# A decoder layer on one core: two block pairs used plainly at the top of the way back, visits staggered by two pairs, weight sums made at once

## The chip, the core and the metric

The kernel runs on one core of a Trainium2 chip. Time is device time in microseconds (us) from the start of one execution to its end; the median of several executions is compared. The core has a matrix engine (PE, with its weight loads PEld), a vector engine (DVE), a scalar engine (ACT), a general engine (POOL) and a synchronising engine (SP). In this kernel SP and POOL also issue the transfers (DMA) between device memory and on-chip memory (SBUF). PE writes its results into eight banks of an accumulator memory (PSUM); DVE and ACT read them from there.

## What is computed

One layer of a decoder, for 512 prompt tokens and 8 × 4 sample tokens, all in 32-bit floats, with width 2048 and an MLP of width 8192. Only the MLP part matters here:

```python
h = rms_norm(x, norm_mix_w)
x = x + mixer(h, ...)                       # projections, convolutions, delta rule, w_out
h = rms_norm(x, norm_ffn_w)
x = x + jnp.square(jax.nn.relu(h @ w_up)) @ w_down    # 2048 -> 8192 -> 2048
return rms_norm(x, final_norm_w)            # and the new states
```

## The kernel before, in words

**Layout.** Activations stand with features on 128 partitions and tokens along the row. The 544 tokens are cut into two halves of 272 (256 of the prompt and 16 samples), so one matmul is 128 × 128 weights against 128 × 272 values. A 2048-wide activation is 16 blocks, or 8 pairs; the 8192-wide one is 64 blocks, or 32 pairs (`NF`), named m = 0 to 31.

**Three matmuls for one product.** PE works in a rounded 32-bit format. Each weight tile and each activation is split into a rounded part (`hi`, by ACT) and a remainder (`lo`, by DVE), and hi·hi + hi·lo + lo·hi are added up in one bank. `weight` (L106 to L122) loads a tile into `w_raw` (two buffers), and splits it into `w_hi` and `w_lo` (three buffers each). A loop called `ahead` calls the load of an item two items before its use.

**Seven products for eight.** For most pairs the MLP takes 2 × 2 blocks of weights (a11, a12, a21, a22) and 2 × 2 blocks of activations (two blocks by two token halves) and forms the four results with seven block products instead of eight, in the way of Strassen and Winograd. Class `Pair` loads the four quads of weights (tiles `w_q`) and makes sums of them on DVE: s1 = a21 + a22 (L1052), a21 = a11 − a21 (L1054), a11 = s1 − a11 (L1055), a12 = a12 − a11 (L1056). The products, numbered 1 to 7, use a11, a12, a22, ... in the order `ORDER` = 1, 2, 5, 6, 7, 3, 4, all through the matmul of L1088. Products 1, 6, 7 and 4 are collected in one bank ("x"), 5 and 3 in another ("z"), 2 in a third ("y"). Since each intermediate sum in x is itself needed, x is read out after 1, 6, 7 and 4 before the next product adds to it. In the function `bilinear` the loads of the next pair's quads are called at product 5.

**Way up.** Pairs 0 to 2 (`N_PLAIN` = 3) are computed plainly (`plain`, one token half at a time). Pairs 3 to 31 go through `bilinear`, 168 matmuls each (7 products × 8 blocks × 3). After each, `block_out` reads out the banks, applies relu and square, and `keep_sums` makes the activation sums that the way back needs and writes them, split, to device memory (`ucd`). A few pairs are stored as they are (`STORED` = 1, 2, 31). Pair 0 is split at once and kept in `u0d`. Pair 2 is read again during pair 8 (`LATER`), and its sums are made then, so that the way back can use it with the others.

**Way back.** First a plain part adds pair 0's share to all 16 blocks of the residual `x2v` (weights `w_d0`, 192 matmuls on L145, additions on DVE L897). Then 29 pairs, 2 to 30 (`KS`), are used in visits: a visit works on one of the 8 pairs of output blocks (m) and on up to `SPAN` = 6 inner pairs, with 7 × n × 3 matmuls for n pairs. The first visits of the eight outputs are staggered (`starts` = 0, 0, 1, 2, 3, 3, 4, 5), so that the inner pairs can be read in through a ring of 8 (`RING`, `fetch`, L1159, issued by POOL); 45 visits in all. Seven additions into `x2v` (L897) follow the seven products of each visit. The weight quads of the visits (`w_q`, from `w_d1`) lie in a pool `qp` that takes the memory of the pools of the way up (`tt`, `sq`), after they are closed. Last, pairs 1 and 31 are used plainly together with the final norm (`w_d2`).

**Order of the work.** The program text gives an order; a scheduler works out the order on each engine at build time from its own model of durations, from a priority (`urgent` raises it) and from when buffers come free. The order on each engine is then fixed: an instruction that has to wait for longer than the model assumed holds up all that stand behind it on that engine.

Of the kernel before, what the change touches and what calls it, by code (L numbers as in the profile page):

```python
# [18 lines left out]
P = 128  # L19
# [20 lines left out]
STORED = [1, 2, NF - 1]  # L40
SPAN, RING = 6, 8
LATER = 8
# [13 lines left out]
def trunk(ctx, tc, a):  # L56
# [835 lines left out]
    u0_d = tile_in(dram, "u0d", [P, 2, 2, 2, HT])  # L892
    uc_d = {m: tile_in(dram, f"ucd{m}", [P, 14, HT]) for m in range(2, NF - 1)}
# [71 lines left out]
    def plain(m, h):  # L965
        t = t_tile("u", "u")
        u = t[:, :2]
        for i in range(2):
            ps = ps_small(HT)
            for j in range(2):  # L970
                with urgent():
                    w = weight(a["w_up"][m, 2 * i + j], 1024)
                for k in range(KT // 2):
                    x = h_c[k][1 + j] if h == 0 else (d_c[k][0][:, j], d_c[k][1][:, j])
                    product({h: ps}, w, k * P, tuple((t, t) for t in x), j == k == 0, j == 1 and k == 7, (h,))
            with urgent():
                S.activation(u[:, i], ps, AF.Relu)
        with urgent():
            S.activation(u, u, AF.Square)
        if m:  # L980
            for i in range(2):
                nc.gpsimd.dma_start(u_d[m][:, 2 * i + 1 - h], u[:, i])
            return
        hi = t[:, 2:4].bitcast(F32R)
        parts_into(hi, u.bitcast(F32R), u)
        for i in range(2):
            nc.gpsimd.dma_start(u0_d[:, 0, i, h], t[:, 2 + i])
            nc.gpsimd.dma_start(u0_d[:, 1, i, h], u[:, i])
# [40 lines left out]
    ORDER = (1, 2, 5, 6, 7, 3, 4)  # L1029

    class Pair:
# [12 lines left out]
        def parts(self, p):  # L1044
            n = self.n
            if p in (1, 2) and self.q is None:
                return weight(self.src[p - 1], n)
            a11, a12, a21, a22 = self.q
            with urgent():
                if p == 5:  # L1050
                    self.s1 = tile_in(rawp, "w_s1", [P, 1024], tag="w_raw")[:, :n]
                    V.tensor_tensor(self.s1, a21, a22, ADD)  # L1052
                elif p == 6:
                    V.tensor_tensor(a21, a11, a21, SUB)  # L1054
                    V.tensor_tensor(a11, self.s1, a11, SUB)  # L1055
                    V.tensor_tensor(a12, a12, a11, SUB)  # L1056
                s = {1: a11, 2: a12, 6: a11, 5: getattr(self, "s1", None), 7: a21, 3: a12, 4: a22}[p]
                hi = tile_in(whip, "w_hi", [P, 1024], F32R)[:, :n]
                lo = tile_in(wlop, "w_lo", [P, 1024], F32R)[:, :n]
                S.activation(hi, s, AF.Copy)  # L1060
                V.tensor_tensor(lo, s, hi.bitcast(F32), SUB)  # L1061
            return hi, lo

    def bilinear(items, early, cs, outs):

        order = [w for w, p in items if p == 5]

        def load(it):
            w, p = it
            if w not in early or p == 5:  # L1070
                w.load()
            if p == 5:
                at = order.index(w)
                for nxt in order[at + 1 : at + 2]:
                    nxt.load()
            return w.parts(p)

        for (w, p), (whi, wlo) in ahead(items, load):
            if p == 1:
                w.ps, w.out = {"x": bank(True)}, outs(w.key)  # L1080
# [34 lines left out]
    def block_out(m):  # L1115
        u = t_tile("u", "u")

        def out(p, ps):
# [15 lines left out]
            if p == 7 and m == LATER:  # L1134
                t = g_tile("u_2", [P, 4, HT])
                nc.sync.dma_start(t, u_d[2])
                keep_sums(2, t)
            if p == 1 and m == NF - 1:
                residual(range(4), nc.sync)
            if p == 5 and m == NF - 1:  # L1140
                for i in range(2):
                    parts = [c_tile(hlp, "u0") for _ in range(2)]
                    for j in range(2):
                        nc.sync.dma_start(parts[j].bitcast(F32), u0_d[:, j, i])
                    u_0.append(tuple(parts))
            if p in (5, 6) and m == NF - 1:
                fetch(p - 5)
# [4 lines left out]
    KS = list(range(2, NF - 1))  # L1152

    def fetch(j):
        n = {4: 4, 5: 0, 6: 0, 7: 0}.get(j % RING, 7)
        n2 = n + {4: 3, 5: 7, 6: 4}.get(j % RING, 0)
# [13 lines left out]
    for j in range(2, 4):  # L1170
        fetch(j)
    x2 = [x2p[i // 2][:, i % 2] for i in range(KT)]
    for q, w in ahead(range(KT // 4), lambda q: weight(a["w_d0"][q], 1024)):
        for j in range(4):
            ob = 4 * q + j
            ps = [bank(True), bank(False)]
            for k in range(2):
                product(ps, w, (2 * j + k) * P, u_0[k], k == 0, k == 1)
            for h in range(2):
                add(x2[ob][:, h], ps[h])  # L1180
    late.close()

# [6 lines left out]
    starts = [SPAN * m // 8 for m in range(8)]  # L1189
    visits = [(m, 0, starts[m]) for m in range(8) if starts[m]]  # L1190
    at = list(starts)
# [7 lines left out]
    for j in range(4, RING):  # L1199
        fetch(j)  # L1200
# [20 lines left out]
    bilinear([(w, p) for w in downs for p in ORDER], (),  # L1221
# [4 lines left out]
    for m in (1, NF - 1):  # L1226
# [102 lines left out]
def _pack(x_prompt, x_sample, state_conv_a, state_conv_qkv, state_delta, norm_mix_w, w_in,  # L1329
# [27 lines left out]
    arr["w_d0"] = wd[:, :, 0:2].reshape(4, 4, P, 2 * P).transpose(0, 2, 1, 3).reshape(4, P, 1024)  # L1357
    w1 = wd.reshape(8, 2, P, NF, 2, P)
    arr["w_d1"] = w1.transpose(0, 1, 4, 2, 3, 5).reshape(8, 4, P, NF * P)
    w2 = wd[:, :, [2 * m + i for m in (1, NF - 1) for i in range(2)]]  # L1360
# [57 lines left out]
```

## Time and profile before

| | |
|---|---|
| median of 3 executions | 2495.59 us (2492.95 to 2500.96) |
| the profiled execution | 2508.89 us, its span 2507.1 us |
| PE | 2435.8 us busy, 97% of the span, 19065 matmuls |
| DVE | 1821.1 us, 73% |
| ACT | 1105.4 us, 44% |
| POOL | 498.3 us, 20% |
| granted PE clock, mean | 0.979 |
| DMA | 400.76 MB, 160 GB/s on average |

A page of the profile gives busy times, the clock that PE was granted, the groups of instructions and the chain of work that ended last. A timeline row gives the start in us, the duration, the engine, the line of the program, the operation, what it writes and reads, the shape, and in brackets how long the engine sat idle before it and what ended that. `xN` at the end of a timeline row means N instructions merged into one row. Matmuls overlap: a row of 0.29 us does not mean that the next one starts 0.29 us later, so pace is read from starts. Some matmul records are missing.

### The profile page before, as it was taken

To read this page: it belongs to the slowest core of one execution; us is meant where nothing else is said; L and a number is where in the kernel's file an instruction comes from. 1 tells how busy PE (TensorE), PEld (TensorE's weight loads), DVE (VectorE), ACT (ScalarE), POOL (GpSimd) and SP (SyncE) were. 2 spreads that over 40 slices of the span, in tenths; PEclk is the share of its full clock that TensorE was granted. 3 is DMA by queue.
4 is the path that set the end of the run, shared out by engine and by line. 5 is a ranking of instruction groups with operands and counts; after the bars stand their busy time and mean duration, and the time that the engine had idled before them with its cause. 6 is when DMAs were issued, how large, how long until landed. Compare 5 with 4: busy or idle time off the path is not lost.

```text
span 2507.1 us, 47369 instructions
## 1 busy us (share of the span) xinstructions
PE 2435.8 (97%) x19065; PEld 2389.9 (95%) x19065; DVE 1821.1 (73%) x2993; ACT 1105.4 (44%) x1628; POOL 498.3 (20%) x783
## 2 busy tenths in 40 slices
PE   8999999999999999999999999999899999999997
PEld 8999999999999899989999999999799999999996
DVE  8676575567557635788888888888488787878795
ACT  5425333332532524565555555555233333333346
POOL 4124113212312303310111111111401111111003
PEclk9999998999998999999999999999899999999998
DMA  6233333332423536565565555556846666566323
GB/s 197 91 106 110 94 101 98 112 97 88 135 88 92 200 106 205 187 195 200 193 228 195 195 194 189 188 190 220 320 127 195 195 195 193 191 194 193 108 84 106
DMA packets 145812, 400.76 MB, mean 160 GB/s; under 512 B 35540, under 2 KB 46456, under 8 KB 145592
## 3 DMA queue, kind: packets, MB, share of 16 engines
q1 hardware_dynamic: 109368, 265.56, 33.7%
q0 software_dynamic: 36224, 132.16, 14.6%
q8 instruction: 150, 2.46, 0.4%
q14 instruction: 70, 0.57, 0.1%
HBM read 318.76 MB, written 78.89 MB: 159 GB/s over the span
## 4 chain that ended last, share of the span: by engine, by line
PE 56%; issue 23%; DVE 9%; DMA 6%; POOL 3%; ACT 2%; SPq 0%; POOLq 0%; DVEq 0%; ACTq 0%
PE ps_big L145 25%; PE ps_s L1088 23%; PE ps_sm L145 3%; DVE w_lo L121 3%; DMA w_raw<-in_w_o_dram 2%; DMA w_raw<-in_w_up_dram 1%; POOL ucd L1106 1%; POOL ucd L1105 1%; DMA w_q<-in_w_d_dram 1%; ACT w_hi L118 1%; DVE xm L560 1%; PE ps_s L145 1%; DVE tm L556 1%; DMA tn<-ti 1%; DVE x2v L897 1%
## 5 line engine op out<-in xcount | busy, mean ns | idle before, releaser
L1088 PE MATMUL ps_s<-uc,w_hi 128*128 128x272 f32 x3248 | 621.1, 291 | 10.8 <-ACT w_hi L1060 8.3
L1060 ACT ACTIVATE w_hi<-w_q 128x768 fp32r<-128x768 f32 (+6 forms) x440 | 382.6, 873 | 544.7 <-PE ps_s L1088 395.3
L1088 PEld LDWEIGHTS ps_s<-uc,w_hi 128*128 128x128 f32 x3248 | 510.8, 189 | 20.4 <-ACT w_hi L1060 11.4
L1061 DVE TENSOR_TENSOR w_lo<-w_q,w_hi 128x768 fp32r<-128x768 f32 (+6 forms) x440 | 434.2, 989 | 61.0 <-ACT w_hi L1060 58.3
L1088 PE MATMUL ps_s<-uc,w_lo 128*128 128x272 f32 x1624 | 462.9, 289 | 0.3
L145 PE MATMUL ps_big<-x_hi,w_hi 128*128 128x272 f32 x1984 | 425.1, 294 | 0.9 <-ACT x_hi L133 0.7
L145 PE MATMUL ps_big<-x_hi,w_lo 128*128 128x272 f32 x1984 | 420.8, 292 | 2.4 <-DVE w_lo L121 2.4
L145 PE MATMUL ps_big<-x_lo,w_hi 128*128 128x272 f32 x1984 | 420.5, 293 | 0.3 <-DVE x_lo L136 0.3
L118 ACT ACTIVATE w_hi<-w_raw 128x1024 fp32r<-128x1024 f32 (+3 forms) x211 | 206.9, 980 | 402.9 <-PE ps_big L145 249.5
L121 DVE TENSOR_TENSOR w_lo<-w_raw,w_hi 128x1024 fp32r<-128x1024 f32 (+3 forms) x211 | 269.8, 1279 | 138.5 <-ACT w_hi L118 135.8
L145 PEld LDWEIGHTS ps_big<-x_hi,w_hi 128*128 128x128 f32 x1984 | 317.2, 190 | 5.0 <-issue 1.4
L145 PEld LDWEIGHTS ps_big<-x_hi,w_lo 128*128 128x128 f32 x1984 | 316.3, 191 | 3.9 <-DVE w_lo L121 3.0
L145 PEld LDWEIGHTS ps_big<-x_lo,w_hi 128*128 128x128 f32 x1984 | 315.9, 191 | 0.9 <-DVE x_lo L136 0.5
L1088 PEld LDWEIGHTS ps_s<-uc,w_lo 128*128 128x128 f32 x1624 | 304.6, 189 | 2.3 <-DVE w_lo L1061 1.9
L1088 PE MATMUL ps_s<-c_hi,w_lo 128*128 128x272 f32 x928 | 267.7, 289 | 2.2 <-DVE w_lo L1061 1.5
L1088 PE MATMUL ps_s<-c_hi,w_hi 128*128 128x272 f32 x928 | 266.6, 287 | 0.5 <-ACT w_hi L118 0.5
L1088 PE MATMUL ps_s<-c_lo,w_hi 128*128 128x272 f32 x928 | 266.3, 287 | 0.0
L1159 POOL DMA_DIRECT2D uc<-ucd x203 | 110.4, 548 | 439.5 <-PE ps_s L1088 411.0
L897 DVE TENSOR_TENSOR x2v<-x2v,ps_s 128x272 f32<-128x272 f32 x347 | 148.6, 434 | 67.5 <-PE ps_s L1088 59.1
L1088 PEld LDWEIGHTS ps_s<-c_hi,w_lo 128*128 128x128 f32 x928 | 174.4, 188 | 3.2 <-DVE w_lo L1061 2.1
L1088 PEld LDWEIGHTS ps_s<-c_hi,w_hi 128*128 128x128 f32 x928 | 174.5, 188 | 0.7 <-ACT w_hi L118 0.7
L1088 PEld LDWEIGHTS ps_s<-c_lo,w_hi 128*128 128x128 f32 x928 | 174.5, 188 | 0.0
(378 smaller groups left out, 4270.7 us busy)
## 6 DMA issues: line engine op xcount, KB each, us to landing
w_q<-in_w_up_dram SPq DMA_DIRECT2D x116, 512.0 KB, 4.3
uc<-ucd POOLq DMA_DIRECT2D x203, 272.0 KB, 5.3
w_raw<-in_w_in_dram SPq DMA_DIRECT2D x106, 512.0 KB, 3.4
w_q<-in_w_d_dram SPq DMA_DIRECT2D x128, 384.0 KB, 3.7
w_raw<-in_w_o_dram SPq DMA_DIRECT2D x32, 512.0 KB, 3.4
ucd<-u_hi POOLq DMA_DIRECT2D x29, 544.0 KB, 5.4
ucd<-tc POOLq DMA_DIRECT2D x29, 544.0 KB, 6.7
w_raw<-in_w_up_dram SPq DMA_DIRECT2D x28, 512.0 KB, 3.6
```

Source lines behind the costliest of these rows:

```text
L118: S.activation(hi[:, c], raw[:, c], AF.Copy)
L121: V.tensor_tensor(lo[:, c], raw[:, c], hi[:, c].bitcast(F32), SUB)
L145: PE.matmul(ps[h], wp[:, c : c + P], x, start=start and i == 0, stop=stop and i == 2)
L556: V.tensor_tensor(t, xm[:, :, j : j + 1].broadcast_to([P, 8, n]), um[:, j : j + 1, j + 1 :].broadcast_to([P, 8, n]), MUL,)
L560: V.tensor_tensor(xm[:, :, j + 1 :], xm[:, :, j + 1 :], t, SUB)
L897: V.tensor_tensor(out, out, ps, ADD)
L1060: S.activation(hi, s, AF.Copy)
L1061: V.tensor_tensor(lo, s, hi.bitcast(F32), SUB)
L1088: PE.matmul(ps, wp[:, k * P : (k + 1) * P], xp, start=p in (1, 2, 5) and k == j == 0, stop=k == len(c) - 1 and j == 2, skip_group_check=True,)
L1105: nc.gpsimd.dma_start(d[:, at : at + n], hi.bitcast(F32))
L1106: nc.gpsimd.dma_start(d[:, 7 + at : 7 + at + n], src)
L1159: nc.gpsimd.dma_start(t.bitcast(F32), uc_d[KS[j]][:, 2 * b : 2 * b + 2])
```

## The change

`N_PLAIN` stays 3, but pairs 0 and 1 are both kept, split, for a plain use at the top of the way back, pair 2 is stored for the end in pair 1's place, and only the 28 pairs 3 to 30 go through visits. The plain part takes 8 weight tiles of 2 output blocks × 4 inner blocks instead of 4 tiles of 4 × 2 (384 matmuls), and it is no longer a stretch of its own: it becomes items of `bilinear`, three ahead of the first visit, two after it, two after the second, one after the third. The first visits start at 0, 0, 2, 2, 4, 4, 6, 6, so there are 42 visits. Pair 2's sums during pair 8 go away, with the reading back of it. In `Pair`, products 5 and 6 change places, and all four weight sums are made at product 6, which now comes third; this holds on the way up and on the way back. The kept parts are read at product 2 of the last pair, eight tiles instead of four. The reads for the ring change their places in the pools accordingly.

```diff
@@ constants
-STORED = [1, 2, NF - 1]
+KEPT = [0, 1]
+STORED = [2, NF - 1]
-LATER = 8
+RAMP = [0, 0, 2, 2, 4, 4, 6, 6]
@@ plain
-        if m:
+        if m not in KEPT:
             for i in range(2):
                 nc.gpsimd.dma_start(u_d[m][:, 2 * i + 1 - h], u[:, i])
             return
         hi = t[:, 2:4].bitcast(F32R)
         parts_into(hi, u.bitcast(F32R), u)
         for i in range(2):
-            nc.gpsimd.dma_start(u0_d[:, 0, i, h], t[:, 2 + i])
-            nc.gpsimd.dma_start(u0_d[:, 1, i, h], u[:, i])
+            nc.gpsimd.dma_start(u0_d[m][:, 0, i, h], t[:, 2 + i])
+            nc.gpsimd.dma_start(u0_d[m][:, 1, i, h], u[:, i])
@@ Pair and bilinear
-    ORDER = (1, 2, 5, 6, 7, 3, 4)
+    ORDER = (1, 2, 6, 5, 7, 3, 4)
...
-                if p == 5:
+                if p == 6:
                     self.s1 = tile_in(rawp, "w_s1", [P, 1024], tag="w_raw")[:, :n]
                     V.tensor_tensor(self.s1, a21, a22, ADD)
-                elif p == 6:
                     V.tensor_tensor(a21, a11, a21, SUB)
                     V.tensor_tensor(a11, self.s1, a11, SUB)
                     V.tensor_tensor(a12, a12, a11, SUB)
...
         def load(it):
             w, p = it
-            if w not in early or p == 5:
+            if p == "plain":
+                return weight(*w.src)
+            if w not in early or p == 6:
                 w.load()
-            if p == 5:
+            if p == 6:
                 at = order.index(w)
                 for nxt in order[at + 1 : at + 2]:
                     nxt.load()
             return w.parts(p)

         for (w, p), (whi, wlo) in ahead(items, load):
+            if p == "plain":
+                w.run((whi, wlo))
+                continue
@@ block_out
-            if p == 7 and m == LATER:
-                t = g_tile("u_2", [P, 4, HT])
-                nc.sync.dma_start(t, u_d[2])
-                keep_sums(2, t)
             if p == 1 and m == NF - 1:
                 residual(range(4), nc.sync)
-            if p == 5 and m == NF - 1:
-                for i in range(2):
+            if p == 2 and m == NF - 1:
+                for i in range(4):
                     parts = [c_tile(hlp, "u0") for _ in range(2)]
                     for j in range(2):
-                        nc.sync.dma_start(parts[j].bitcast(F32), u0_d[:, j, i])
+                        nc.sync.dma_start(parts[j].bitcast(F32), u0_d[i // 2][:, j, i % 2])
                     u_0.append(tuple(parts))
-            if p in (5, 6) and m == NF - 1:
-                fetch(p - 5)
+            if p in (6, 5) and m == NF - 1:
+                fetch(6 - p)
@@ ring
-    KS = list(range(2, NF - 1))
+    KS = list(range(N_PLAIN, NF - 1))
     def fetch(j):
-        n = {4: 4, 5: 0, 6: 0, 7: 0}.get(j % RING, 7)
-        n2 = n + {4: 3, 5: 7, 6: 4}.get(j % RING, 0)
+        n = {3: 0, 4: 0, 5: 0, 7: 4}.get(j % RING, 7)
+        n2 = n + {3: 7, 4: 7}.get(j % RING, 0)
@@ top of the way back
-    for j in range(2, 4):
-        fetch(j)
     x2 = [x2p[i // 2][:, i % 2] for i in range(KT)]
-    for q, w in ahead(range(KT // 4), lambda q: weight(a["w_d0"][q], 1024)):
-        for j in range(4):
-            ob = 4 * q + j
-            ps = [bank(True), bank(False)]
-            for k in range(2):
-                product(ps, w, (2 * j + k) * P, u_0[k], k == 0, k == 1)
-            for h in range(2):
-                add(x2[ob][:, h], ps[h])
     late.close()
+    class Plain:
+        def __init__(self, q):
+            self.q, self.src = q, (a["w_d0"][q], 1024)
+        def run(self, w):
+            for j in range(2):
+                ob = 2 * self.q + j
+                ps = [bank(True), bank(False)]
+                for k in range(4):
+                    product(ps, w, (4 * j + k) * P, u_0[k], k == 0, k == 3)
+                for h in range(2):
+                    add(x2[ob][:, h], ps[h])
...
-    starts = [SPAN * m // 8 for m in range(8)]
-    visits = [(m, 0, starts[m]) for m in range(8) if starts[m]]
-    at = list(starts)
+    visits = [(m, 0, RAMP[m]) for m in range(8) if RAMP[m]]
+    at = list(RAMP)
...
-    for j in range(4, RING):
+    for j in range(2, RING):
         fetch(j)
...
-    bilinear([(w, p) for w in downs for p in ORDER], (),
+    items = [[(w, p) for p in ORDER] for w in downs]
+    plains = [(Plain(q), "plain") for q in range(8)]
+    items[0] = plains[:3] + items[0] + plains[3:5]
+    items[1] += plains[5:7]
+    items[2] += plains[7:]
+    bilinear([it for part in items for it in part], (),
              lambda key: [combos(key[1][1] + k) for k in range(key[1][2])], down_out)
@@ last
-    for m in (1, NF - 1):
+    for m in STORED:
```

More of the change, by code (lines that the diff above doesn't have):

```diff
@@ L891, in trunk @@
     u_d = {m: tile_in(dram, f"ud{m}", [P, 4, HT]) for m in STORED}
-    u0_d = tile_in(dram, "u0d", [P, 2, 2, 2, HT])
-    uc_d = {m: tile_in(dram, f"ucd{m}", [P, 14, HT]) for m in range(2, NF - 1)}
+    u0_d = [tile_in(dram, f"u0d{m}", [P, 2, 2, 2, HT]) for m in KEPT]
+    uc_d = {m: tile_in(dram, f"ucd{m}", [P, 14, HT]) for m in range(N_PLAIN, NF - 1)}
     def add(out, ps):
@@ L1064, in bilinear @@
     def bilinear(items, early, cs, outs):
-        order = [w for w, p in items if p == 5]
+        order = [w for w, p in items if p == 6]
         def load(it):
             w, p = it
-            if w not in early or p == 5:
+            if p == "plain":
+                return weight(*w.src)
+            if w not in early or p == 6:
                 w.load()
-            if p == 5:
+            if p == 6:
                 at = order.index(w)
@@ L1356, in _pack @@
     wd = _blocks(w_down[0])
-    arr["w_d0"] = wd[:, :, 0:2].reshape(4, 4, P, 2 * P).transpose(0, 2, 1, 3).reshape(4, P, 1024)
+    arr["w_d0"] = wd[:, :, 0:4].reshape(8, 2, P, 512).transpose(0, 2, 1, 3).reshape(8, P, 1024)
     w1 = wd.reshape(8, 2, P, NF, 2, P)
     arr["w_d1"] = w1.transpose(0, 1, 4, 2, 3, 5).reshape(8, 4, P, NF * P)
-    w2 = wd[:, :, [2 * m + i for m in (1, NF - 1) for i in range(2)]]
+    w2 = wd[:, :, [2 * m + i for m in STORED for i in range(2)]]
     arr["w_d2"] = w2.reshape(8, 2, P, 512).transpose(0, 2, 1, 3).reshape(8, P, 1024)
```

## The prediction

> **What bounds the kernel now.** The page's engine totals come first, then the matrix engine's (PE's) timeline for its pace, then the windows for the place of the lost time.
>
> ```profile
> span 2507.1 us, 47369 instructions
> PE 2435.8 (97%) x19065; PEld 2389.9 (95%) x19065; DVE 1821.1 (73%) x2993; ACT 1105.4 (44%) x1628; POOL 498.3 (20%) x783
> ```
>
> PE is occupied 97% of the span, so only matmul count and PE's gaps can move the end. Its undisturbed pace is read from the first four products of the last pair on the way up, 96 matmuls in a row, of which these are the first and the last:
>
> ```profile
> 1740.12 0.29 PE L1088 MATMUL ps_s<-c_hi,w_hi 128*128 128x272 f32 x1
> ...
> 1751.98 0.29 PE L1088 MATMUL ps_s<-c_hi,w_lo 128*128 128x272 f32 x1
> ```
>
> 11.86 us over 95 steps: 0.1248 us per matmul. Any window's length less its matmuls times 0.1248 is its loss. Columns below: stretch, length, then busy time and count of PE and of the others, granted clock, DMA share, GB/s.
>
> ```profile
> 1248.50:1312.20 63.70, 61.12 (x470) 60.15 (x469) 51.68 (x63) 35.10 (x44) 8.69 (x16) 0.97 0.62 219
> 1312.20:1376.00 63.80, 63.80 (x507) 63.19 (x506) 52.95 (x61) 37.16 (x45) 6.52 (x12) 1.00 0.57 194
> 1376.00:1741.50 365.50, 365.50 (x2895) 362.02 (x2894) 303.79 (x345) 213.14 (x259) 36.93 (x68) 1.00 0.55 193
> 1762.80:1847.00 84.20, 69.95 (x463) 65.44 (x462) 51.93 (x125) 21.15 (x41) 25.03 (x46) 0.90 0.73 261
> 1847.00:2360.00 513.00, 513.00 (x4050) 508.42 (x4049) 412.85 (x585) 190.78 (x226) 79.84 (x147) 1.00 0.57 181
> 2360.00:2437.30 77.30, 74.17 (x561) 71.02 (x559) 66.46 (x140) 32.20 (x59) 0.00 (x0) 1.00 0.30 85
> ```
>
> In order: around the delayed sums of pair 2 the loss is 63.7 − 470 × 0.1248 = 5.0 us, in the next stretch of equal length 0.5, in the steady way up 4.2 over 17 pairs, in the top of the way back (plain product and the five short visits) 26.4, in the steady visits 7.6 over 32, in the last short visits 7.3. The top of the way back is the largest, and its granted clock is 0.90.
>
> **The change, part by part.**
>
> *More matmuls.* A pair used plainly costs 8 × 48 matmuls per two pairs; the visits take 8 × 28 × 21 = 4704 instead of 8 × 29 × 21 = 4872, the plain part 384 instead of 192. Net +24 × 0.1248 = **+3.0**.
>
> *Order 1, 2, 6, 5, 7.* Products 6 and 7 use one bank, and 7 may start only when 6 has been copied out. They stand next to each other now; PE bridges the copy with matmuls of product 3, then pauses:
>
> ```profile
> 1562.26 0.28 PE L1088 MATMUL ps_s<-d_lo,w_hi 128*128 128x272 f32 x1
> 1562.53 0.39 PE L1088 MATMUL ps_s<-d_hi,w_hi 128*128 128x272 f32 x1
> 1562.76 0.29 PE L1088 MATMUL ps_s<-d_lo,w_hi 128*128 128x272 f32 x1
> ```
>
> ```profile
> 1562.09 0.38 ACT L1121 ACTIVATE u<-ps_s 128x272 f32<-128x272 f32 x1
> ```
>
> The copy ends at 1562.47 and the next matmul starts at 1562.53; the two steps take 0.50 instead of 0.25, so 0.25 us per pair. With 5 between 6 and 7 the copy has 24 × 0.1248 = 3.0 us, or 2.2 in a visit of six, against under 1.5 us from the end of 6 to the end of the copy. Products 7 and 4 stand so today, one product apart, and no gap is there. On the way up 28 × 0.25 = **−7.0** (bounds 0 and −7.5), in the visits 7.6 × 30/32 = **−7.0** (bounds 0 and −8).
>
> *All four weight sums ahead of product 6.* The third product now waits for four sums instead of one. Today's order on the vector engine (DVE), and the rounding on the scalar engine (ACT) that starts the third product:
>
> ```profile
> 1545.60 1.23 DVE L1061 TENSOR_TENSOR w_lo<-w_q,w_hi 128x1024 fp32r<-128x1024 f32 x1 [0.58 <-ACT w_hi L1060]
> ...
> 1547.09 1.22 DVE L1055 TENSOR_TENSOR w_q<-w_s,w_q 128x1024 f32<-128x1024 f32 x1
> ...
> 1549.37 1.22 DVE L1052 TENSOR_TENSOR w_s<-w_q 128x1024 f32<-128x1024 f32 x1
> 1550.50 1.22 DVE L1061 TENSOR_TENSOR w_lo<-w_s,w_hi 128x1024 fp32r<-128x1024 f32 x1
> 1551.63 1.22 DVE L1056 TENSOR_TENSOR w_q<-w_q 128x1024 f32<-128x1024 f32 x1
> 1552.77 1.22 DVE L1054 TENSOR_TENSOR w_q<-w_q 128x1024 f32<-128x1024 f32 x1
> ```
>
> ```profile
> 1549.15 1.06 ACT L1060 ACTIVATE w_hi<-w_s 128x1024 fp32r<-128x1024 f32 x1 [1.06 <-PE ps_s L1088]
> ```
>
> ```profile
> 1549.02 0.29 PE L1088 MATMUL ps_s<-c_hi,w_hi 128*128 128x272 f32 x1
> ```
>
> ACT rounds s1 at 1549.15 while DVE writes the next s1 at 1549.37: s1 and L1054 are made a whole pair ahead. Product 6 then hangs on L1055 alone, which needs the first product's `w_lo` and ends at 1548.31; the third product's buffer comes free later, at 1549.02, when the pair's first product starts on PE. Cost **0** under cover of that lead; without it, rival D. The first pair of the way up has no lead, and pays today:
>
> ```profile
> 1157.59 0.39 PE L1088 MATMUL ps_s<-d_hi,w_lo 128*128 128x272 f32 x1 [1.98 <-DVE w_lo L1061]
> ```
>
> There three sums move ahead of the third product, 3 × 1.135 = 3.4 us of DVE time, but as much of it as today must be done before the fifth; the wait comes earlier and is not larger in total: 0, bounds ±2.5.
>
> *Pair 2's sums dropped on the way up.* They used a quad buffer and `tc`:
>
> ```profile
> 1267.34 0.44 DVE L1007 TENSOR_TENSOR tc<-u 128x272 f32<-128x272 f32 x1 [2.93 <-DMA ucd<-tc]
> ...
> 1281.24 1.23 DVE L1052 TENSOR_TENSOR w_s<-w_q 128x1024 f32<-128x1024 f32 x1 [1.38 <-DMA w_q<-in_w_up_dram]
> ```
>
> ```profile
> 1283.66 0.39 PE L1088 MATMUL ps_s<-d_hi,w_lo 128*128 128x272 f32 x1 [2.08 <-DVE w_lo L1061]
> ...
> 1287.61 0.43 PE L1088 MATMUL ps_s<-d_hi,w_lo 128*128 128x272 f32 x1
> ```
>
> The loss goes from 5.0 to the neighbour's 0.5: **−4.5** (bounds −3 and −5). These rows also show what a wait costs behind itself: after 2.08 us idle PE steps at 0.226 (1283.66 to 1283.89) until 1287.8, some 2 us more. The Trainium skill, "TensorE: Matmul & The Clock Gate", section "What's actually happening", puts the halving of the clock behind an idle window of about 3.4 us. Here 2.08 us is enough, so the measurement decides; by the page the waits left at the top would be 2 us cheaper, and the sum −35.
>
> *Pair 1 kept.* It adds, per half of the tokens, a rounding, a subtraction and two more writes on POOL's queue:
>
> ```profile
> 1114.17 0.72 DVE L925 TENSOR_TENSOR u<-u 128x544 fp32r<-128x544 f32 x1
> ```
>
> ```profile
> 1113.40 0.66 ACT L924 ACTIVATE u<-u 128x544 fp32r<-128x544 f32 x1
> ```
>
> Between 0 (both steps in idle time between weight splits) and 2 × (0.66 + 0.72) = 2.8 bare, taken as **+1.0**: DVE has gaps there, but some splits will stand behind the new steps. POOL's extra writes have nothing behind them that PE waits for before the top of the way back. The four more loads of kept parts on SP go out at product 2 of the last pair, ahead of the plain weights; that traffic is in the next term.
>
> *The top of the way back.* Now a plain stretch of 24 us, then visits of 1, 2, 3, 3, 4, 5; afterwards three plains (18 us), a visit of 2, two plains, a visit of 2, two plains, a visit of 4, a plain, a visit of 4, then sixes. The reads of stored sums keep their order on POOL (0, 1, the residual, 2 and on); 6 and 7 now wait for the kept `u` until the last plain, but their first use is the ninth visit, and behind them stand only later reads: 0.
>
> ```profile
> 1762.80 0.66 PE L145 MATMUL ps_s<-u,w_hi 128*128 128x272 f32 x4
> ```
>
> ```profile
> SPq L1042 <- DMA ud<-u: 11.0, 1, 11.0
> ```
>
> ```profile
> 1774.11 1.48 DVE L897 TENSOR_TENSOR x2v<-x2v,ps_s 128x272 f32<-128x272 f32 x4
> 1783.85 0.29 DVE L1052 TENSOR_TENSOR w_s<-w_q 128x128 f32<-128x128 f32 x1 [8.27 <-DMA uc<-ucd]
> ```
>
> ```profile
> 1784.87 1.40 PE L145 MATMUL ps_s<-u,w_hi 128*128 128x272 f32 x4 [6.06 <-DVE x2v L897]
> 1786.06 0.66 PE L145 MATMUL ps_s<-u,w_lo 128*128 128x272 f32 x2
> ...
> 1805.44 0.52 PE L1088 MATMUL ps_s<-uc,w_hi 128*128 128x272 f32 x2 [3.12 <-ACT w_hi L1060]
> ...
> 1818.04 0.52 PE L1088 MATMUL ps_s<-uc,w_hi 128*128 128x272 f32 x2 [2.21 <-ACT w_hi L1060]
> ```
>
> SP's first weight quads wait until the last pair's `u` is written (`qp` lies where `u` lay), and all later loads of SP stand behind them; DVE, at the first sum, waits for them until 21.0 us after the first plain matmul (1783.85 − 1762.8); the residual additions behind it leave PE without banks for 6.06 us. The change keeps this cause: `u` is written at the same point of POOL's queue, and the first quads are twice as large. But the three plains are 144 × 0.1248 = 18.0 us of PE work in six blocks; two of them are added before DVE stops, and the four banks of each kind hold the rest. The first visit can start at 21.0 plus one split of 0.4 and the step to PE, say 22: about 4 us idle, plus the 2 of slow clock seen above. A visit of 2 costs DVE 11 weight passes and 7 additions against 42 × 0.1248 = 5.2 us of PE:
>
> ```profile
> 1807.50 1.09 DVE L1061 TENSOR_TENSOR w_lo<-w_q,w_hi 128x256 fp32r<-128x256 f32 x3
> ```
>
> 1.09/3 and 1.48/4 give 11 × 0.36 + 7 × 0.37 = 6.6: 1.4 us each, 2.8. Each plain behind a visit of 2 waits 1.06 + 1.23 for its 1024-wide split, with 1.5 us of PE work as cover: 0.8, twice. Together 6 + 2.8 + 1.6 = 10.4, say 11: **−15** (bounds: −23 if the quads land in time, −3 if the short visits lose as now).
>
> *The end.* Visits 5, 5, 4, 3, 2, 2, 1 become 4, 4, 4, 4, 2, 2. Two twos at 1.4 and the final splitting wait of today
>
> ```profile
> 2434.29 0.52 PE L1088 MATMUL ps_s<-uc,w_hi 128*128 128x272 f32 x2 [1.18 <-ACT w_hi L1060]
> ```
>
> make 4.0 against 7.3: **−3.5** (bounds 0 and −6). What follows, pair 2 in pair 1's place, has equal work: 0.
>
> Sum: 3 − 7 − 7 − 4.5 + 1 − 15 − 3.5 = **−33**. The profiled execution took 2508.89 us, 13.3 above the median; I take the difference off the median 2495.59: **2463**.
>
> **Rivals.**
> *B, the top moves its waits.* DMA runs at 261 GB/s over this window, and early sums may sit in DVE's queue ahead of plain additions at each of the three returns. The Trainium skill, "TensorE: Matmul & The Clock Gate", section "Architectural detail", calls DVE's queue strictly first in, first out; the 8.27 us row agrees. Then −15 becomes −3: 2475. Against it: loads of plain weights give transfers 6 to 12 us more between visits.
> *C, the pause is not the bank's.* The −7s vanish: 2477. Against it: the copy's end and the restart lie 0.06 us apart.
> *BC, both:* 2489, within the bound below.
> *D, product 6 is late in every pair (slower).* If DVE makes all four sums after the second `w_lo` (ending 1549.37): 4 × 1.135 + 1.06 + 1.23 ends at 1556.2, while PE wants it at 1555.26 (two products after 1549.02, third matmul). 1.0 us in 28 pairs and 38 visits, +66: 2529. It turns slower from 0.5 us. Against it: the lead above.
>
> **How the numbers follow.** Forecast 0.54, B 0.16, C 0.14, BC 0.09, D 0.07. Faster is the first three, 0.84; no change (0.3% is 7.5 us, about what a measurement tells) is BC; slower is D. The range 2446 to 2484 takes the forecast with its terms' bounds, B and C, and leaves out BC, D and the far ends.
>
> **What would show it.** Right: no 0.25 us pause per pair, no waits around 1268 to 1288, PE loss at the top near 11 us with one wait of about 4 before the first visit, 19089 matmuls. Wrong: `w_s` waits of several us repeated between plains (B), pauses left at product 7 (C), PE waiting for `w_lo` at the third product of each pair (D).

## The result, and the profile after

The changed kernel takes 2471.08 us (median of 4 executions, 2468.36 to 2478.74) against 2498.28 us for the kernel before on the same chip (4 executions): the ratio is 0.9894, with a 95% interval of 0.987 to 0.9918. That is 27.2 us less. 33 us less had been forecast, from a base of 2495.59.

The page of the changed kernel, its span and engine totals:

```profile
span 2471.1 us, 47391 instructions
PE 2407.6 (97%) x19089; PEld 2375.8 (96%) x19089; DVE 1803.2 (73%) x2939; ACT 1095.5 (44%) x1611; POOL 494.7 (20%) x776
```

PE has the 24 matmuls more that were counted, and 28.2 us less of occupied time: a PE that waits inside a product partly counts as busy, so the loss is read from windows again (length less matmuls × 0.1248). The windows of the changed kernel, cut at the same events as before; columns: stretch, length, then busy time and count of PE, PEld, DVE, ACT and POOL, granted clock, DMA share, GB/s:

```profile
0.00:1043.60 1043.60, 1019.96 (x8156) 999.12 (x8156) 670.49 (x1379) 409.02 (x701) 290.80 (x414) 0.98 0.39 124
1043.60:1124.10 80.50, 76.81 (x580) 74.55 (x579) 62.47 (x101) 49.74 (x76) 10.34 (x19) 0.98 0.63 206
...
1150.40:1742.70 592.30, 591.18 (x4716) 589.88 (x4715) 490.94 (x559) 343.41 (x420) 66.80 (x123) 1.00 0.57 200
1742.70:1841.01 98.31, 89.10 (x675) 87.21 (x673) 58.61 (x118) 25.40 (x40) 27.25 (x50) 0.95 0.71 255
1841.01:2312.03 471.02, 468.75 (x3725) 467.09 (x3724) 379.29 (x533) 175.37 (x207) 75.96 (x140) 1.00 0.57 185
2312.03:2401.63 89.60, 88.71 (x701) 88.00 (x700) 79.95 (x151) 38.37 (x63) 0.00 (x0) 1.00 0.30 88
```

The stretches of the kernel before that the prediction did not show (everything ahead of the MLP, the plain pairs, and the way up behind its first pair):

```profile
0.00:1052.50 1052.50, 1029.21 (x8155) 1008.21 (x8156) 672.52 (x1379) 409.37 (x701) 290.15 (x414) 0.97 0.39 123
1052.50:1133.70 81.20, 76.14 (x581) 73.25 (x580) 60.96 (x99) 48.80 (x74) 8.21 (x15) 1.00 0.62 199
...
1160.00:1762.80 602.80, 598.92 (x4715) 592.59 (x4715) 493.56 (x564) 347.68 (x422) 71.15 (x131) 1.00 0.57 200
```

Loss in us by stage; the rows of the first pair of the way up and of the end come out of the same view. The columns behind the first two are a second execution of the changed kernel (run e11) and one experiment that returns below:

| stage | before | after | after, e11 | e10, steps of one pair | forecast of the difference |
|---|---|---|---|---|---|
| ahead of the MLP (unchanged code) | 34.8 | 25.7 | 27.3 | 24.1 | 0 |
| plain pairs 0 to 2 | 8.7 | 8.1 | 9.2 | 9.8 | +1.0 |
| way up, first pair | 6.2 | 6.1 | 8.1 | 6.5 | 0 |
| way up, the rest | 14.4 | 3.7 | 2.2 | 3.6 | −11.5 |
| top of the way back | 26.4 | 14.1 | 14.3 | 15.2 | −15 |
| steady visits | 7.6 | 6.1 | 4.3 | 1.4 | −7 |
| last short visits | 7.3 | 2.1 | 1.7 | 3.4 | −3.5 |
| end | 20.4 | 20.5 | 20.5 | 21.3 | 0 |

The two profiled spans lie 36.0 us apart, 9.1 of it ahead of the first line that the change touches. That stage's code is the same in all runs, and its loss lay between 18.4 us (e6) and 34.8, so it is left out. The other stages give −30.3, and +3.0 for the 24 matmuls makes −27.3 (with e11's profile −30.7 + 3.0 = −27.7), close to the difference of the medians, 27.2. That it is this close is partly luck: the two profiles of the changed kernel say that a single stage can be trusted to about 2 us.

**The top.** The changed kernel's PE waits around the first visit and the first short ones, from its timeline:

```profile
1762.92 0.52 PE L1093 MATMUL ps_s<-uc,w_hi 128*128 128x272 f32 x2 [1.85 <-ACT w_hi L1060]
1764.54 0.52 PE L1093 MATMUL ps_s<-uc,w_hi 128*128 128x272 f32 x2 [0.39 <-ACT w_hi L1060]
1769.54 0.59 PE L1093 MATMUL ps_s<-uc,w_lo 128*128 128x272 f32 x1 [4.48 <-DVE w_lo L1061]
1772.41 0.82 PE L1093 MATMUL ps_s<-uc,w_hi 128*128 128x272 f32 x2 [0.90 <-DVE x2v L898]
...
1834.85 0.49 PE L1093 MATMUL ps_s<-uc,w_hi 128*128 128x272 f32 x2 [1.47 <-DVE x2v L898]
```

The same on DVE and on SP's queue (waits of SP: what it waited for, total, times, longest), and what the transfers did from 1735 to 1780 (queue issues with KB each and median us to landing):

```profile
1767.57 0.42 DVE L1053 TENSOR_TENSOR w_s<-w_q 128x256 f32<-128x256 f32 x1 [4.25 <-DMA w_q<-in_w_d_dram]
```

```profile
SPq L1043 <- DMA ud<-u: 15.1, 1, 15.1
```

```profile
DMA packets 5885, 17.48 MB, mean 388 GB/s; under 512 B 921, under 2 KB 1938, under 8 KB 5882
...
w_q<-in_w_d_dram SPq DMA_DIRECT2D x8, 128.0 KB, 8.7
```

Waits of 7.6 us in four places stand around the first visit. The first visit starts 20.2 us after the first plain matmul, and the first sum 24.9 us after it (1767.57 − 1742.69). There is no wait of 6 us for banks any more, and of the short visits only one wait of 1.47 is left.

**The steady visits.** One place of a new kind, out of the visit around 2020: POOL's ring reads, DVE, and PE.

```profile
2016.34 1.09 POOL L1160 DMA_DIRECT2D uc<-ucd  x2 [51.63 <-PE ps_s L1093]
...
2025.94 2.71 POOL L1160 DMA_DIRECT2D uc<-ucd  x5 [1.34 <-PE ps_s L1093]
```

```profile
2021.96 0.96 DVE L1053 TENSOR_TENSOR w_s<-w_q 128x768 f32<-128x768 f32 x1 [1.31 <-DMA w_q<-in_w_d_dram]
...
2024.58 0.43 DVE L898 TENSOR_TENSOR x2v<-x2v,ps_s 128x272 f32<-128x272 f32 x1
```

```profile
2025.15 0.49 PE L1093 MATMUL ps_s<-uc,w_hi 128*128 128x272 f32 x2 [0.48 <-DVE x2v L898]
```

With outputs staggered by two pairs, two places of the ring come free in one visit: the rows from the first shown to the last hold 2, 2, 2, 3 and 5 reads of 272 KB, 14 in 12 us, and before them there is none for 51.63 us. The next weight quads travel among them. DVE is held 1.31 us at the first sum by one of them, the addition at 2024.58 stands behind it in program order, and PE waits for the bank that it empties.

### The profile page after: what moved, and what is told of

Read it like the earlier page. It is cut to its first block, busy times and chain, and to the rows that moved or that the text cites. A ratio compares the mean times of both kernels' runs of the same rounds, so it can differ in the third digit from the quotient of the medians.

```text
span 2471.1 us, 47391 instructions
## 1 busy us (share of the span) xinstructions
PE 2407.6 (97%) x19089; PEld 2375.8 (96%) x19089; DVE 1803.2 (73%) x2939; ACT 1095.5 (44%) x1611; POOL 494.7 (20%) x776
## 4 chain that ended last, share of the span: by engine, by line
PE 80%; DVE 8%; DMA 7%; ACT 3%; issue 2%; SPq 0%; POOL 0%; DVEq 0%; ACTq 0%; POOLq 0%
PE ps_s L1093 45%; PE ps_big L146 27%; DVE w_lo L122 2%; PE ps_sm L146 2%; DMA w_raw<-in_w_up_dram 2%; DMA w_raw<-in_w_o_dram 2%; DMA w_q<-in_w_d_dram 2%; PE ps_s L146 1%; ACT w_hi L119 1%; DVE w_lo L1061 1%; PE ps_sm L738 1%; DVE x L937 0%; DVE x2v L1250 0%; PE ps_sm L532 0%; DMA tn<-ti 0%
## 5 line engine op out<-in xcount | busy, mean ns | idle before, releaser
L1060 ACT ACTIVATE w_hi<-w_q 128x768 fp32r<-128x768 f32 (+3 forms) x422 | 375.3, 889 | 554.5 <-PE ps_s L1093 461.4
L1093 PE MATMUL ps_s<-uc,w_hi 128*128 128x272 f32 x3136 | 594.6, 289 | 7.9 <-DVE x2v L898 3.9
L1093 PEld LDWEIGHTS ps_s<-uc,w_hi 128*128 128x128 f32 x3136 | 492.5, 189 | 11.7 <-ACT w_hi L1060 6.8
L1061 DVE TENSOR_TENSOR w_lo<-w_q,w_hi 128x768 fp32r<-128x768 f32 (+3 forms) x422 | 424.8, 1008 | 63.0 <-ACT w_hi L1060 61.4
L1093 PE MATMUL ps_s<-uc,w_lo 128*128 128x272 f32 x1568 | 451.5, 288 | 4.5 <-DVE w_lo L1061 4.5
L122 DVE TENSOR_TENSOR w_lo<-w_raw,w_hi 128x1024 fp32r<-128x1024 f32 (+3 forms) x215 | 275.1, 1280 | 149.0 <-ACT w_hi L119 144.8
L1093 PEld LDWEIGHTS ps_s<-uc,w_lo 128*128 128x128 f32 x1568 | 296.0, 189 | 4.9 <-DVE w_lo L1061 4.9
L898 DVE TENSOR_TENSOR x2v<-x2v,ps_s 128x272 f32<-128x272 f32 x326 | 139.8, 433 | 68.0 <-PE ps_s L1093 57.4
```

The costliest lines, as they stand in the source:

```text
L122: V.tensor_tensor(lo[:, c], raw[:, c], hi[:, c].bitcast(F32), SUB)
L898: V.tensor_tensor(out, out, ps, ADD)
L1093: PE.matmul(ps, wp[:, k * P : (k + 1) * P], xp, start=p in (1, 2, 5) and k == j == 0, stop=k == len(c) - 1 and j == 2, skip_group_check=True,)
```

## The experiments

**The order alone (e1).** The kernel before, with products 5 and 6 exchanged and all four sums at product 6. The call for the next pair's loads moves with product 6, and pair 0's kept parts are read at product 2.

```diff
-    ORDER = (1, 2, 5, 6, 7, 3, 4)
+    ORDER = (1, 2, 6, 5, 7, 3, 4)
-                if p == 5:
+                if p == 6:
                     ... s1
-                elif p == 6:
                     ... the other three sums
```

> The kernel before with one part of the change: products in the order 1, 2, 6, 5, 7, 3, 4 and all four weight sums at product 6, on both ways. Pair 2 still has its sums made late, the plain part and the first visits are as before. Theory A (the pause at product 7 is the wait for the bank, and what went wrong in the visits of the changed kernel is that the weight quads come late there, because two inner pairs are read into the ring at a time): the pauses vanish on both ways, no new waits come in the visits, where one inner pair is read at a time: loss in the steady visits from 7.6 to about 1, on the way up from 14 to about 7, together about -13 us against before. Theory B (the new order itself leaves the additions too little room, one product, so that any late quad stops PE): the way up gains 7, the visits keep 5 or more of their 7.6 us, with PE waiting for additions into x2v, together about -9 us. Theory C (the sums at once are late in every pair): slower than before.

2487.27 us, ratio 0.9969 (0.9946 to 0.9992). Its windows of the way up and of the steady visits, and all of PE's waits in the latter (total, times, longest):

```profile
1156.10:1753.30 597.20, 593.55 (x4723) 592.36 (x4722) 495.17 (x565) 345.48 (x424) 70.36 (x130) 1.00 0.57 202
```

```profile
1837.50:2343.33 505.83, 505.49 (x4033) 505.09 (x4034) 414.05 (x584) 190.56 (x226) 79.97 (x147) 1.00 0.59 184
```

```profile
PE ps_s L1087 <- DVE x2v L897: 0.3, 1, 0.3
```

Way up: 597.2 − 4723 × 0.1248 = 7.8 against 14.4, so 6.6 less (pair 2's late sums are still in it). Steady visits: 505.83 − 4033 × 0.1248 = 2.5 against 7.6, so 5.1 less. The pauses went on both ways, as they should if they were the bank's, and making four sums at once costs nothing where each pair has a pair's lead. The last short visits lose 4.3 instead of 7.3, the top 27.4 instead of 26.4.

**The old order in the changed kernel (e2).** The mirror image: everything of the change but the order.

```diff
-    ORDER = (1, 2, 6, 5, 7, 3, 4)
+    ORDER = (1, 2, 5, 6, 7, 3, 4)
     ... sums at products 5 and 6 as before
```

> The changed kernel with the old order of products (1, 2, 5, 6, 7, 3, 4) and the sums at products 5 and 6. Both theories: the pause of 0.25 us comes back in each pair on the way up, +7 us. In the visits theory A expects the pauses back and late quads besides, loss 8 to 11 us there; theory B expects 7 to 8 as in the kernel before. Together +8 to +12 us against the changed kernel.

2485.94 us, ratio 0.9957 (0.9939 to 0.9976). Way up and steady visits, and PE's waits in the latter:

```profile
1151.60:1749.10 597.50, 596.41 (x4715) 590.55 (x4714) 489.83 (x558) 346.09 (x420) 67.14 (x125) 1.00 0.56 198
```

```profile
1847.41:2329.33 481.92, 477.51 (x3757) 472.37 (x3756) 382.66 (x538) 176.27 (x209) 75.87 (x140) 1.00 0.56 182
```

```profile
PE ps_s L1094 <- DVE x2v L898: 2.6, 4, 1.6
PE ps_s L1094 <- ACT w_hi L1061: 1.7, 2, 0.9
```

Way up 9.1, some 5 us more than with the new order. Steady visits 481.92 − 3757 × 0.1248 = 13.0: 5.4 us more than in the kernel before, which has the same order. Beside the pauses there are waits here that the kernel before does not have, so the staggering by two brings a loss of its own, whatever the order. The whole is 14.9 us above the changed kernel by medians (2485.94 − 2471.08), where the order was forecast at 14.

**Pair 2's sums put back (e3).** The changed kernel, with the reading and summing of pair 2 during pair 8 again. It does this work for nothing, nobody uses the result.

```diff
-    uc_d = {m: ... for m in range(N_PLAIN, NF - 1)}
+    uc_d = {m: ... for m in range(2, NF - 1)}
...
+            if p == 7 and m == 8:
+                t = g_tile("u_2", [P, 4, HT])
+                nc.sync.dma_start(t, u_d[2])
+                keep_sums(2, t)
```

> The changed kernel with pair 2's sums put back on the way up (read again and summed during pair 8, written, and not used by the way back). The prediction's term: +4.5 us against the changed kernel, as waits of PE for w_lo of 0.5 and 2 us and slow clock behind them near that pair. Rival: with the new order the disturbance is absorbed, +1 us or less.

2479.83 us, ratio 0.9929 (0.9899 to 0.9959). The stretch around pair 8, and the wait in it:

```profile
1251.00:1267.00 16.00, 13.13 (x93) 12.91 (x92) 9.81 (x14) 6.87 (x9) 2.16 (x4) 0.89 0.63 220
```

```profile
1260.35 0.39 PE L1093 MATMUL ps_s<-d_hi,w_hi 128*128 128x272 f32 x1 [2.87 <-ACT u L1126]
```

16 − 93 × 0.1248 = 4.4: the prediction's 4.5. The size is the same, the wait is not: the waits for `w_lo` that had been expected do not come, and PE waits for a bank instead. Its copy on ACT stands behind a rounding (L925, from 1258.19) that ACT could start only after 4.81 idle us. The way up behind its first pair loses 8.5 us, 4.8 more than in the changed kernel. The median is 8.8 us above, but the two intervals overlap, so the size rests on the stage.

**All plain products ahead of the first visit (e4).**

```diff
-    items[0] = plains[:3] + items[0] + plains[3:5]
-    items[1] += plains[5:7]
-    items[2] += plains[7:]
+    items[0] = plains + items[0]
```

> The changed kernel with all eight plain items ahead of the first visit. If the gain at the top comes from threading plains between visits: the short visits follow each other without cover, their quads land late as in the kernel before (waits of 2 to 3 us with slow clock), loss at the top back to 20 or more, +6 us or more against the changed kernel. If it comes from the sizes of the visits and the longer plain part: the wait of 4.5 us before the first visit goes away under 48 us of plain work, the two visits of two lose 1.4 us each, loss at the top under 10, -4 us or better.

2469.68 us, ratio 0.99 (0.9867 to 0.9934), and 14.1 us lost in the top, as with the threading. Only the places differ:

```profile
1784.77 1.24 PE L146 MATMUL ps_s<-u,w_hi 128*128 128x272 f32 x4 [2.65 <-ACT w_hi L119]
1809.72 1.27 PE L1093 MATMUL ps_s<-uc,w_hi 128*128 128x272 f32 x4 [3.67 <-ACT w_hi L1060]
```

With 48 us of plain work in front (384 × 0.1248), the first visit's weights are there in time, but a plain weight tile comes late: its load is issued behind the first quads (at 1764.83) and takes 16.1 us to land. The first short visits, now without cover between them, wait 3.67 us. Neither theory had this result. The threading is worth nothing by itself here. Nor is the gain lost with the old order (e2, 15.4 lost in the top), with pair 2's sums put back (e3, 15.1) or with steps of one pair (e6 below, 14.9). What remains as its source is the second plain pair; that it was not taken away alone leaves this argued.

**The last pair's activations written by SP, early (e5).**

```diff
-                nc.gpsimd.dma_start(u_d[m], u)
+                with urgent():
+                    nc.sync.dma_start(u_d[m], u)
```

> The changed kernel; the stored u of the last pair (and of pair 2's place among the stored ones) is written by SP with priority instead of by POOL behind the ring's reads. Theory: the wait of 4.5 us at the first visit comes from the first weight quads waiting for this write, which stands in POOL's queue behind reads; the write then lands some 6 us earlier, loss at the top from 14.0 to 7 to 9, -5 to -7 us against the changed kernel. Rival: the transfers themselves are the limit there (255 GB/s in that stretch), the quads land at the same time, -2 us or less.

2476.05 us, ratio 0.9909 (0.989 to 0.9927), top 15.7: no gain. SP's waits for the values and for the write, and the landing of the first quads (1735 to 1780, as above):

```profile
SPq L1137 <- ACT u L1129: 8.9, 1, 8.9
```

```profile
SPq L1043 <- DMA ud<-u: 6.2, 1, 6.2
```

```profile
DMA packets 5896, 17.67 MB, mean 393 GB/s; under 512 B 954, under 2 KB 1978, under 8 KB 5893
...
w_q<-in_w_d_dram SPq DMA_DIRECT2D x8, 128.0 KB, 9.8
```

SP's wait for the write shrank from 15.1 to 6.2 us, but SP, which now issues the write itself, waits 8.9 us for `u` before it. Counted from the first plain matmul (1740.25 here, 1742.69 in the changed kernel), the write goes out 0.6 us sooner, and the first quads leave 1.2 us later (after 13.4 us instead of 12.2) and take 9.8 us to land instead of 8.7. The theory was wrong at its root: the write did not stand behind the reads. In the changed kernel, ACT's end of `u` and POOL's write:

```profile
1747.05 1.06 ACT L119 ACTIVATE w_hi<-w_raw 128x1024 fp32r<-128x1024 f32 x1 [5.46 <-DMA w_raw<-in_w_d_dram]
...
1748.43 1.11 ACT L1129 ACTIVATE u<-u 128x1088 f32<-128x1088 f32 x1
```

```profile
1749.84 0.54 POOL L1136 DMA_DIRECT2D ud<-u  x1 [1.87 <-DVE x2v L898]
```

The write is issued 0.3 us after `u` is finished (1749.54). What delays `u` is ACT's order: the rounding of a plain tile stands ahead of the last relu and square, and waits 5.46 us for that tile's weights. In the kernel before, the square stands ahead of that rounding:

```profile
1763.43 1.11 ACT L1124 ACTIVATE u<-u 128x1088 f32<-128x1088 f32 x1
```

It ends 1.74 us after the first plain matmul (1762.80) there, and 6.85 us after it in the changed kernel. A run with the square first was not made, so what that would bring is open.

In steady visits quads three times that size land in 3.3 us (median of 120). Between 1735 and 1780 the transfers move 388 to 393 GB/s, against 185 in the steady visits, and about two thirds of those bytes are the ring's reads (42 of 272 KB). So the time is the rival's, while its cause, that transfers share a full system there, fits but is not shown. Whether fewer bytes there would shorten the top was not tried.

**Stagger by one pair (e6, and again as e10, beside the changed kernel e11).**

```diff
-RAMP = [0, 0, 2, 2, 4, 4, 6, 6]
+RAMP = [0, 0, 1, 2, 3, 4, 5, 6]
```

> The changed kernel with the first visits staggered by one pair (starts 0, 0, 1, 2, 3, 4, 5, 6) instead of by two, plains threaded as there. If the loss left in the visits (6.0 us) comes from two inner pairs being read into the ring at a time, it falls to about 2.5 as in the run with the new order alone; the top gets visits of 1, 2 and 3 (+3 us) and the end of 3, 2, 1 (+3): about +2 us together. If it comes from something else in the changed kernel, the visits keep 6 and the whole is +6.

> The changed kernel with its first visits staggered by one pair (0, 0, 1, 2, 3, 4, 5, 6), all else the same; more rounds, beside the changed kernel itself on the same chip. Theory: reading two pairs of the ring in one visit is what makes weight quads late in the steady visits, worth some 4 us there (loss 6.0 against 1.8) and given back in part by shorter first visits: 0 to 4 us under the changed kernel, loss of the steady visits under 3 us again. Rival: the visits' small loss in the first such run was chance: loss 5 to 7 us and the same time or more than the changed kernel.

> The changed kernel, unchanged, as the yardstick for the other run: 2468 to 2479 us, loss of the steady visits 5 to 7 us, loss at the top of the way back about 14 us, loss on the way up under 4 us. If the stages of one execution scatter by more than 2 us from those of the first profile, readings of the stages below that size are not to be trusted.

e6: 2472.22 us, ratio 0.9893 (0.9866 to 0.9919). e10: 2475.45, 0.9903 (0.9887 to 0.9919). e11: 2471.52, 0.989 (0.9868 to 0.9912). The steady visits of e10 and of e11:

```profile
1841.21:2309.53 468.32, 468.32 (x3741) 468.24 (x3740) 382.35 (x537) 176.24 (x208) 76.39 (x140) 1.00 0.59 184
```

```profile
1843.81:2313.13 469.32, 468.03 (x3726) 466.97 (x3725) 379.99 (x534) 175.35 (x207) 75.97 (x140) 1.00 0.57 186
```

Stepping by one loses 1.4 us there (1.9 in e6), with no PE wait at all; stepping by two loses 4.3 (6.1 in the first profile of the changed kernel). DMA's GB/s in 40 slices of that window, of the changed kernel and of e6, show what differs:

```profile
GB/s 136 100 74 105 281 276 91 347 199 171 328 103 135 82 88 344 209 138 346 133 229 301 104 104 100 116 309 208 157 343 104 247 290 98 102 114 140 343 140 172
```

```profile
GB/s 99 102 135 141 202 262 200 221 221 266 184 190 101 101 181 213 239 245 205 203 236 241 159 75 99 215 224 206 260 203 232 207 267 134 75 99 258 193 189 104
```

Nearly the same bytes (87.2 and 86.4 MB) come in peaks of about 345 by two and of about 265 by one. The longest landing of a weight quad there is 7.0 and 6.2 us by two (changed kernel, e11) and 5.2 and 5.7 by one (e6, e10), and DVE's longest wait for one 1.7 and 1.6 us against 0.8 and 0.7. Yet the whole is no faster: e10's median lies 3.9 us above e11's, where 0 to 4 us below had been expected, and the intervals overlap. The gain is given back, as had been expected for e6: the top, the last short visits and the end together lose 39.2 us in e6 (14.9 + 2.6 + 21.7) and 39.9 in e10, against 36.7 and 36.5 in the changed kernel's two profiles. Steps of two pairs cost some 3.5 us in the steady visits and give back some 3 in the rest.

**The second of two ring reads put off by a visit (e7).**

```diff
-                    if last_use[j] == v:
+                    if last_use[j] + j % 2 == v:
```

> The changed kernel with the second of each two ring reads put off by one visit, and nothing else. Theory A (two reads at a time make the next weight quads late): loss in the visits from 6.0 to about 2.5, -3.5 us against the changed kernel; top and end as there. Rival: the waits stay (6.0) or the reads put off come too late for the visit that needs them, and PE waits for uc (+2 or more).

2477.29 us, ratio 0.9923 (0.9896 to 0.9949); the steady visits lose 5.4, and the intervals of this run and of the changed kernel overlap. POOL's reads at the place that was shown for the changed kernel:

```profile
2020.87 1.08 POOL L1160 DMA_DIRECT2D uc<-ucd  x2 [51.64 <-PE ps_s L1093]
...
2030.24 2.70 POOL L1160 DMA_DIRECT2D uc<-ucd  x5 [1.12 <-PE ps_s L1093]
```

The edit did not spread the reads. The rows hold 2, 2, 2, 3 and 5 reads again, 14 in 12 us, behind a pause of 51.64 us, and the other places in the steady visits look the same in both kernels. A call that stands one visit later in the program text did not make these reads start later; each row still starts as PE's products free the buffers. So the run says nothing about the remedy. That the spacing of the reads is the whole difference between steps of two and of one is argued, not shown.

**The four sums at the last moment (e9).** The first sum is fixed in program order on DVE, so that all four stand between the second product's split and product 6's.

```diff
-                    V.tensor_tensor(self.s1, a21, a22, ADD)
+                    tc.keep_in_program_order(V.tensor_tensor(self.s1, a21, a22, ADD))
```

> The changed kernel with the first of the four sums held in program order on the vector engine, behind everything issued before it, so that all four stand right before product 6's split and the lead of a pair is gone. The prediction's rival D: 1.0 us of waiting in each of 28 pairs and 38 visits, +30 to +66 us, as PE waits for w_lo or w_hi at the third product. If the lead is not what hides the sums: no change within 5 us.

2770.76 us in one execution. The way up, DVE in one pair of it, and PE:

```profile
1154.10:2011.50 857.40, 667.93 (x4737) 652.99 (x4736) 514.37 (x563) 349.75 (x422) 71.98 (x133) 0.85 0.39 142
```

```profile
1527.65 1.22 DVE L1053 TENSOR_TENSOR w_s<-w_q 128x1024 f32<-128x1024 f32 x1
...
1532.56 1.22 DVE L1061 TENSOR_TENSOR w_lo<-w_q,w_hi 128x1024 fp32r<-128x1024 f32 x1
```

```profile
1501.81 0.59 PE L1093 MATMUL ps_s<-c_hi,w_hi 128*128 128x272 f32 x1 [6.77 <-ACT w_hi L1060]
1532.53 0.59 PE L1093 MATMUL ps_s<-c_hi,w_hi 128*128 128x272 f32 x1 [6.77 <-ACT w_hi L1060]
```

The way up loses 857.4 − 4737 × 0.1248 = 266 us. A pair takes 30.72 us from wait to wait instead of 168 × 0.1248 = 20.97: 6.77 of waiting, and 2.98 more because PE then steps slowly. So the "nothing" for the four sums holds only by the lead of a pair, and without it the price is 9.75 us a pair on the way up. In the steady visits it is far lower: they lose 27.9 us (498.32 − 3769 × 0.1248) instead of 6.1, 0.7 us for each of some 30 visits.

## Why the prediction was mostly right, point by point

**The size.** 2471.08 lies in the range, 8 us above the forecast. 2.7 of that is the base: the kernel before measured 2498.28 here, 2495.59 there. The other 5.4 lie in the terms below, the visits first.

**More matmuls, +3.0.** 19089, as counted.

**Order on the way up −7.0, pair 2's sums −4.5.** Together −10.7 (−12.2 with e11) against −11.5. Alone, the order brought 6.6 (e1) or 5.4 (e2), the sums 4.8 (e3). Right, with the cause: rival C, that the pause is not the bank's, falls with e1, where the order and the place of the sums changed and the pauses went.

**Order in the visits, −7.0: the step that failed.** Its mechanism holds: e1 got 5.1 of it. But the prediction priced the order against visits that otherwise stayed as they were, and the same change makes the ring's reads come in pairs. That cost 5.4 us with the old order (e2 against the kernel before) and some 3.5 with the new one (the changed kernel's two profiles against e6 and e10), and left −1.5 (−3.3 with e11). The prediction looked at the places of POOL's reads in its queue and at when their data are used, and found 0; what it left out was how many of them fall into one visit and what else is in transit then. That the loss goes with steps of two is shown (with the new order, six profiled executions that have them, those of the changed kernel, e3, e4, e5, e7 and e11, lose 4.3 to 6.1 us, and the two with steps of one 1.4 and 1.9); that it is the bunched reads that make the quads late is argued.

**Four sums at once, 0.** Right; and the lead named as its cover is what pays for it (e9). Rival D's price was far too low: +66 was worked out from 1.0 us a pair, as if DVE were free right after the second split. In e9 the sums stand behind the activation sums and an addition, and each wait is followed by slow matmuls: 9.75 us a pair on the way up; in the visits the 1.0 us was near what came (0.7). The chance of D was small for the right reason, but its time, where it holds fully, lies almost 290 us beyond the range.

**First pair of the way up, 0.** 6.2 and 6.1 (8.1 in e11): right within the scatter.

**Pair 1 kept, +1.0.** The plain pairs lose 8.1 and 9.2 against 8.7: no cost that these runs can show.

**The top, −15.** −12.3 and −12.1, with the mechanism as described, but put together otherwise. The wait for the first quads stayed and the plains of the second kept pair carry it. But the first sum came after 24.9 us, not 21.0. The prediction kept the write of `u` at its place in POOL's queue, and it stayed there, yet it left out that ACT makes `u` and takes a plain tile's rounding first: counted from the first plain matmul, `u` is ready 5.1 us later than in the kernel before. A faster write (4.8 us instead of 8.7) makes most of that good, so that the first quads leave 1.2 us later (12.2 instead of 11.1); from there to the first sum it takes 12.7 us instead of 10.0. (The row quoted for that wait in the kernel before names a read of the ring as what ended it; the sum reads only quads, and the changed kernel's row names them.) The waits at the first visit are 7.6 us instead of 4. The slow steps behind them, 2 us in the forecast, are 2.7, from a narrower window of the changed kernel (columns as in the other windows):

```profile
1769.50:1775.50 6.00, 5.07 (x19) 4.54 (x20) 5.03 (x15) 1.97 (x5) 3.24 (x6) 0.50 1.03 388
```

19 matmuls in 6.00 us at half the clock, 0.90 of it a wait, where 19 × 0.1248 = 2.4 would do. The short visits and the plains behind them, priced at 4.4, take the remaining 3.8. Rival B, that the top only moves its waits, is refuted for the change as a whole (26.4 to 14.1), yet it describes what happened in e4, which moved the waits and kept the sum.

The prediction also read the slow steps too roughly. Here is the kernel before again, behind the wait that it quoted, and the place in e3 with a wait of 2.87 us (PE's timelines, the first slow step and the first quick one behind):

```profile
1284.66 0.43 PE L1088 MATMUL ps_s<-d_hi,w_hi 128*128 128x272 f32 x1
...
1288.04 0.29 PE L1088 MATMUL ps_s<-d_lo,w_hi 128*128 128x272 f32 x1
```

```profile
1261.71 0.40 PE L1093 MATMUL ps_s<-d_lo,w_hi 128*128 128x272 f32 x1
...
1265.24 0.29 PE L1093 MATMUL ps_s<-c,w_lo 128*128 128x272 f32 x1
```

In both PE runs at full pace for 1.0 and 1.4 us after the wait (which ended at 1283.66 and at 1260.35) and only then slowly, for 3.4 us (1284.66 to 1288.04) and 3.5 us (1261.71 to 1265.24). The start is not always late: behind e4's wait of 2.65 us the slow steps begin at once, at 1784.77, and last 3.75 us (to 1788.52); behind 4.48 us (changed kernel, 1769.54) and 6.77 us (e9) they begin at once too. The Trainium skill, "TensorE: Matmul & The Clock Gate", section "What's actually happening", describes a free-running window of about 3.4 us over which PE's activity is watched; the length of the slow stretch and its changing start agree with that. That a whole window must be idle does not agree: 2.08, 2.65 and 2.87 us were enough here. The wait of 1.47 us at 1834.85 is followed by no slow step. So such a wait costs itself and 1.5 to 1.8 us more: the 16 steps of e3 from 1261.71 on take 3.53 us instead of 2.00, and the 16 of e4 from 1784.77 on 3.75.

**The end, −3.5.** −5.2 and −5.6 (the prediction's own figures, 7.3 to 4.0, make −3.3). e1 shows where the excess is from: its last visits, unchanged in their sizes, went from 7.3 to 4.3 by the order alone, a gain that the prediction had not counted at this place.

## What to carry to other kernels

When one step regroups visits, work out not only when each transfer may start but how many start together, and which loads are in transit then; a queue of its own did not keep a burst from making another queue's loads late (longest landing 7.0 us against 5.2). An engine's slack covers an added step only by the lead with which it runs: name the lead, and price the case without it with all that stands ahead on that engine and with the slow steps after the wait. Before a transfer is moved to another queue, look at when its data are ready: in e5 the write was held by ACT and not by its queue. And look in the trace whether an edit moved what it was meant to move: e7's reads started as before.

## What the runs showed of the hardware that was not expected

Unchanged code scatters more than what is to be measured: the 8156 matmuls ahead of the MLP lost between 18.4 and 34.8 us in the profiled executions. Two spans must therefore be compared by stages.

A transfer's time to landing grew far more than its size says: 128 KB quads took a median of 8.7 to 9.8 us at 388 to 393 GB/s, and 384 KB quads 3.3 us at 185 GB/s.

PE's slow stretch can come late: behind three waits of 2.1 to 2.9 us PE ran at about half its pace for 3.4 to 3.75 us, once at once and twice only after 1.0 and 1.4 us at full pace. Who looks only at the first matmuls after a wait can take the wait to be all of its price.
